# Attention values of a head group: four runs of one head each, or one run with two heads alternating in the two column halves

## Chip, cores and metric

One core of a Trainium2 chip runs the whole program. The metric is the device time in microseconds, as the median of three runs. The chip's engines are named as in the profile: PE (matrix multiply; PEld is its weight load), DVE (vector), ACT (activation), POOL, and SP, which issues most loads.

## What is computed

One layer of a transformer trunk for 256 tokens of width 1024: a sparse-attention mixer, a cross attention to 256 memory tokens, and a convolutional feed-forward network. The change lies in the mixer, which has 16 heads of width 64 in 4 groups. The four heads of a group share keys and values. Cut to what matters:

```python
p_cmp = masked_softmax(einsum('bghtd,bngd->bghtn', qg, k_cmp), cmp_end[None, :] <= t[:, None])
o_cmp = einsum('bghtn,bngd->btghd', p_cmp, v_cmp)
...
p_sel = masked_softmax(einsum('bghtd,bgtkd->bghtk', qg, k_g), ...)
o_sel = einsum('bghtk,bgtkd->btghd', p_sel, v_g)
...
p_win = masked_softmax(einsum('bghtd,bkgd->bghtk', qg, k_w), wmask)
o_win = einsum('bghtk,bkgd->btghd', p_win, v_w)
o = g_blk[..., 0:1] * o_cmp + g_blk[..., 1:2] * o_sel + g_blk[..., 2:3] * o_win
return o.reshape(B, S, D_MODEL) @ w_out
```

With 256 tokens all four key blocks are selected and the window is longer than the sequence, so the selected and the window branch both reduce to causal attention, each with its own keys and values.

## The kernel before, in words

The weights stream from memory in halves of 128x1024 (`load_half`, L108, issued by SP). Each half is split into a high part on ACT (L116) and a low part on DVE (L120), and each weight product takes three PE passes (`mm3`, L183 to L185). At most four halves are in flight as `raw`, six as `hi` and as `lo`.

The attention is cut into units `(g, t)`: a group of four heads and a tile of 128 queries. `UNITS` (L887) lists the eight units, `heads` (L888) the 32 heads `(g, t, i)` in that order. A head of query tile 0 sees 128 keys in two branches (256 columns, two blocks), one of tile 1 sees 256 keys (512 columns, four blocks). A head runs through these steps of the class `Head` (L767):

- `scores`, PE, L779 and L780, into a bank of the tag `S` (two banks);
- `biggest`, DVE, L790: minus the scores and their largest, into `pp` (three buffers);
- `exp`, ACT, L796, twice (one per branch);
- `weigh`, DVE, L801 to L804: the division by the sum and the gate;
- `transposed`, PE, L810, one transpose per block, into a bank of the tag `PT` (two banks);
- `copied`, ACT, L814, from that bank into the tile `pT`, of which there are two buffers;
- `values`, PE, L827, one `matmul` per block: the stationary operand is the block's values, 128 keys by 64 columns, and the moving one is 128 columns of `pT`;
- `summed`, L834: after the unit's fourth head, ACT (L188) and DVE (L192) split the output bank into `oT`.

The output of a unit is one bank of the tag `O` (two banks), 256 columns wide. An even head of the group goes to partitions 0 to 63, an odd one to partitions 64 to 127, the first two heads to columns 0 to 127 and the last two to the rest. So the values of an even head occupy one half of the PE array's columns and those of an odd head the other half. Ahead of the first head's values, two products over all 128 columns (L821) put the compressed branch of all four heads into the bank. All operands here are float32: each such `matmul` is issued as two pairs of a weight load and a matmul, so the 96 calls of L827 stand as 192 matmuls in the profile.

The loop at L893 staggers the heads: in step `n` it issues the scores of head `n`, the weighing of head `n-1`, the transposes and copy of head `n-2`, and the values of head `n-3`. Between them `advance` (L878) takes steps from other products: the remaining queries, the memory's keys (`pmk`) and values (`pmv`). The output projection that follows (`residual`, L917, `pr_out` in the profile) uses `oT`.

That is the program's order, and it isn't the order on the engines. In this stretch only SP and POOL keep the written order (`M2`, L891). For PE, ACT and DVE a planner fixes one order per engine when the kernel is built: it goes by costs that it models, prefers what stands earlier in the program, and takes whatever is ready in its model. On the chip each engine then follows that fixed order and waits where it must.

Of the kernel before, what the change touches and what calls it, by code (L numbers as in the profile page):

```python
# [17 lines left out]
P = 128  # L18
# [16 lines left out]
# columns of the per-partition constants  # L35
# [7 lines left out]
def trunk_kernel(ctx: ExitStack, tc: tile.TileContext, a, out):  # L43
# [60 lines left out]
    def load_half(i):  # L104
        """Load the next half of chunk i."""
        h = len(raws.setdefault(i, []))
        raw = wpool.tile([P, NHALF], F32, tag="raw", name=f"raw{i}_{h}", bufs=RAW)
        nc.sync.dma_start(raw, chunks[i][0][:, h * NHALF:(h + 1) * NHALF])  # L108
        raws[i].append(raw)

    def split_half(i, lo=None):
        """Split the next half of chunk i, or the one part of it."""
        if not lo:
            h = len(his.setdefault(i, []))
            his[i].append(wpool.tile([P, NHALF], F32R, tag="hi", name=f"hi{i}_{h}", bufs=NBUF))
            nc.scalar.activation(his[i][h], raws[i][h], AF.Copy)  # L116
        if lo is not False:
            h = len(parts.setdefault(i, []))
            t = wpool.tile([P, NHALF], F32R, tag="lo", name=f"lo{i}_{h}", bufs=NBUF)
            nc.vector.tensor_tensor(t, raws[i][h], f(his[i][h]), op=ALU.subtract)  # L120
            parts[i].append((his[i][h], t))

    def half(i, h, k):
        """Half h of chunk i, of which the rows-tile k comes next; what follows has been split up to
        AHEAD halves on."""
        if not order:
            order.extend((n, j) for n, c in enumerate(chunks) for j in range(c[1] // NHALF))
        at = order.index((i, h))
        at += min(AHEAD, RAMP + (at - 4) // RS)
        while state["hi"] < len(order) and state["hi"] <= at:  # L130
            n, j = order[state["hi"]]
            if len(raws.get(n, [])) == j:
                load_half(n)
            split_half(n, False)
            state["hi"] += 1
        while state["lo"] < state["hi"] and (state["lo"] < at or k >= SKEW):
            split_half(order[state["lo"]][0], True)
            state["lo"] += 1
        return parts[i][h]

    def wtile(i, k, c, n):
        """hi and lo of rows-tile k, columns c:c+n of a chunk [P, 8, 256]."""
        hi, lo = half(i, k // 4, k % 4)
        o = (k % 4) * 256 + c
        return hi[:, o:o + n], lo[:, o:o + n]

    def wrow(i, k):
        """hi and lo of rows-tile k (of 4) of a chunk [P, 4, 512]."""
        hi, lo = half(i, k // 2, 2 * (k % 2))
        o = (k % 2) * 512  # L150
        return hi[:, o:o + 512], lo[:, o:o + 512]

    # the order in which the chunks are used
# [26 lines left out]
    def mm3(ps, lw, rx, start, stop):  # L180
        """Three float32r passes of a float32 product: hi hi, hi lo, lo hi."""
# [14 lines left out]
    def split(*items):  # L196
        """hi + lo = src (* scale), each of float32r, for (hi, lo, src, scale): all of one bank,
        which one engine reads at a time."""
# [6 lines left out]
    def sumsq(src, nm, dve=False):  # L205
        """The sum of the squares of src over D."""
# [8 lines left out]
    def partial(parts_, nm):  # L215
        """eps and the sums of squares but the last."""
# [20 lines left out]
    def across(rs, row, nm, tag="O"):  # L237
        """rs [tokens, tiles] as a row of tokens, the same in all partitions."""
# [39 lines left out]
    def proj_ws(ps, ci, ct, pair, t=None):  # L278
        """ps[128 columns of the weights, tokens] of chunk ci, column tile ct."""
# [3 lines left out]
    def proj_ws_steps(ps, ci, ct, pair):  # L283
        """The same in steps, between which other products can go."""
# [4 lines left out]
    def proj_as(ps, c0, pair, t):  # L289
        """ps[tokens of t, 512 columns] from the two chunks c0, c0 + 1."""  # L290
# [3 lines left out]
    # products of a stream come in steps, between which other pieces of work go  # L294
# [10 lines left out]
    def between(stream, start):  # L305
        """The steps of the stream, and of the work that starts at the given ones."""
# [17 lines left out]
    # the memory's keys and values, at the other end of the memory  # L324
# [4 lines left out]
    with tc.tile_pool(name="attn", bufs=1, reuse_waits="tile") as at:  # L329
# [10 lines left out]
        hT = act_pair("hT", "aA")  # L340
        # the root mean squares of the tokens scale what comes out of the products with x
        xT = act.tile([P, KT, S], F32, tag="aB_hi", name="xT")
        rs_x = at.tile([P, NT], F32, name="rs_x")
        with tc.manual_schedule():
# [11 lines left out]
            # the table of the functions is loaded, and the clock of the PE array rises, while the first  # L356
            # loads arrive
# [24 lines left out]
        # queries: rows of hi and lo of one head  # L382
        QS = at.tile([P, G, HPG, S], F32R, name="QS")
        with tc.tile_pool(name="cmp", bufs=1, side="right", reuse_waits="tile") as cp:
# [8 lines left out]
            def rms():  # L393
                """The root mean squares of the tokens: per token, and as a row; then the values."""
# [19 lines left out]
            # ---- compressed keys' and values' inputs: [(parity, d), position pair, part, (chunk, group)],  # L414
            # for the first and the second half of a block; the last column is the position embedding ----
# [71 lines left out]
            gel = cp.tile([P, 2, 2, NC], F32, name="gel")  # L487

            def hidden(j, then):
                """Twice the gelu of the hidden layer, [hidden, (block, group)]."""  # L490
# [47 lines left out]
            def gated():  # L538
                """The gates."""
# [76 lines left out]
            def compressed_values():  # L616
                # block-diagonal over the four heads of a group
# [39 lines left out]
        with tc.tile_pool(name="aq", bufs=1, reuse_waits="tile") as aq:  # L657
# [18 lines left out]
            def mem_values(h):  # L676
                """The values of head h."""
# [87 lines left out]
            # all of the four blocks are selected, and the window is longer than the sequence, so the  # L765
            # masks of these two branches are the causal one
            class Head:  # L767
# [14 lines left out]
                def biggest(self):  # L782
# [5 lines left out]
                    # minus the scores (scaled by the queries' rms), and minus their largest  # L788
# [23 lines left out]
                def copied(self):  # L812
                    self.pT = aq.tile([P, 512], F32, tag="pT", name=f"pT{self.name}", bufs=2)
                    nc.scalar.activation(self.pT[:, :self.w], self.pt[:, :self.w], AF.Copy)  # L814

                def values(self):
                    g, t, i = self.g, self.t, self.i
                    if i == 0:
                        Os[g, t] = bank("O", f"O{g}{t}")
                        for m in range(2):  # L820
                            nc.tensor.matmul(Os[g, t][:, m * P:(m + 1) * P], Vc[:, g, m, :], pcT[:, g, t, :],  # L821
                                             start=m == 0, stop=False, skip_group_check=True)
                    O = Os[g, t]
                    po = O[(i % 2) * DK:(i % 2) * DK + DK, (i // 2) * P:(i // 2 + 1) * P]
                    nb = 2 * (1 + t)
                    for blk in range(nb):
                        nc.tensor.matmul(po, V[:, blk // 2, blk % 2, g, :], self.pT[:, blk * P:(blk + 1) * P],  # L827
                                         start=False, stop=i == HPG - 1 and blk == nb - 1,
                                         skip_group_check=True)
# [32 lines left out]
            def fill():  # L862
                """The steps of other products."""
# [24 lines left out]
            heads = [Head(g, t, i) for g, t in UNITS for i in range(HPG)]  # L888
            for t in range(NT):
# [27 lines left out]
    def residual(c0, pair, nm, norm, man):  # L917
        """x += pair @ w; norm(t, sums of squares of the halves) of each tile of tokens."""
# [23 lines left out]
    with tc.tile_pool(name="cross", bufs=1, reuse_waits="tile") as cr:  # L942
# [8 lines left out]
        def cross_q(ci, ps):  # L951
            """The queries of head ci, transposed."""
# [7 lines left out]
        def cross_p(h):  # L960
            """The probabilities of head h, transposed."""
# [37 lines left out]
        # the first heads' queries by tiles of tokens, then transposed  # L999
# [33 lines left out]
    with tc.tile_pool(name="ffn", bufs=1, reuse_waits="tile") as fp:  # L1033
# [5 lines left out]
        # the first pairs of column tiles by tiles of tokens, then transposed  # L1039
# [42 lines left out]
        def add_pd(pd, t, h, c0, c1):  # L1082
            """x += pd for columns c0:c1 of half h, and the sum of squares."""
# [6 lines left out]
        for h in range(2):  # L1090
            # (tokens, columns) of the accumulators
# [27 lines left out]
def _rows(w, c0, c1):  # L1119
    """[K, c0:c1] -> [128, K / 128, c1 - c0]: rows of a tile on the partitions."""  # L1120
# [4 lines left out]
def _stationary(w):  # L1125
    """Chunks of 256 columns and all rows."""
# [3 lines left out]
def _moving(w):  # L1130
    """Chunks of 512 columns and 512 rows, the columns outermost."""
# [4 lines left out]
def _moving_r(w):  # L1136
    """The same, the rows outermost."""
# [71 lines left out]
```

## Time and profile before

| what | value |
|---|---|
| device time, median of 3 runs | 483.68 us (483.61 to 483.83) |
| span of the profiled execution, from its first to its last instruction | 481.1 us |
| PE busy | 464.0 us, 96% |
| DVE busy | 328.6 us, 68% |
| ACT busy | 294.0 us, 61% |
| values (L827), busy on PE, 192 matmuls | 27.4 us |

The page of the profile gives the profiled execution's span; the device time of the runs holds a little more than a span, what lies ahead of the first and behind the last instruction. An instruction that PE shows as busy overlaps its neighbours, since matmuls are pipelined: two matmuls can start 0.11 us apart and be shown with 0.27 us each. What a matmul costs is therefore read from the distance between starts, not from its shown length.

### The profile page before, as it was taken

What the parts mean: (1) busy time and instruction counts of PE and PEld (TensorE: products, weight loads), DVE (VectorE), ACT (ScalarE), POOL (GpSimd) and SP (SyncE); (2) the same over time, 40 slices, a digit from 0 to 9 for tenths busy, and PEclk for the clock granted to TensorE, in tenths of its full rate; (3) what the DMA queues carried; (4) which work ended last, traced back from release to release, by engine and by line L of the source; (5) the groups of instructions that cost most, each with busy time, mean ns of one, the idle gap of its engine ahead of it and who ended that gap; (6) DMA issues with size and microseconds to landing.
All of it is one profiled execution on the core that took longest, in us unless ns stands there. A gap on an engine that the chain in (4) does not pass through costs nothing.

```text
span 481.1 us, 8742 instructions
## 1 busy us (share of the span) xinstructions
PE 464.0 (96%) x3278; PEld 423.7 (88%) x3278; DVE 328.6 (68%) x716; ACT 294.0 (61%) x613; POOL 37.5 (8%) x82
## 2 busy tenths in 40 slices
PE   7999598999999999999999999999999999999994
PEld 4899598899988777789999889999999999888884
DVE  4799879688777668485563395897777777744413
ACT  5889769666677567484555275766666666534401
POOL 4122101211100000010000010000000000000203
PEclk9999978999999999999999999999999999999998
DMA  7987785432222200264533453765555555654502
GB/s 265 359 272 254 216 281 199 164 131 89 104 74 88 89 1 1 90 201 158 196 104 117 143 178 124 235 211 190 188 190 176 177 176 176 215 179 137 169 0 89
DMA packets 22074, 77.05 MB, mean 160 GB/s; under 512 B 2704, under 2 KB 3088, under 8 KB 22032
## 3 DMA queue, kind: packets, MB, share of 16 engines
q1 hardware_dynamic: 21312, 74.65, 45.6%
q10 hardware_dynamic: 720, 1.84, 1.1%
q8 instruction: 26, 0.43, 0.4%
q14 instruction: 16, 0.13, 0.1%
HBM read 75.43 MB, written 1.05 MB: 159 GB/s over the span
## 4 chain that ended last, share of the span: by engine, by line
PE 85%; DMA 6%; DVE 3%; ACT 2%; issue 2%; SPq 0%; POOLq 0%; ACTq 0%; DVEq 0%; POOL 0%
PE up L183 8%; PE up L185 8%; PE up L184 8%; PE O L827 5%; PE pd L183 4%; PE pd L184 4%; PE pd L185 4%; DMA raw<-in_w_q 3%; PE pt L810 3%; DMA raw<-in_w_vsvw 2%; PE pmk L183 2%; PE pmk L185 2%; PE pmv L185 2%; PE pr_out L183 2%; PE pmv L183 2%
## 5 line engine op out<-in xcount | busy, mean ns | idle before, releaser
L120 DVE TENSOR_TENSOR lo<-raw,hi 128x1024 fp32r<-128x1024 f32 x134 | 164.0, 1230 | 64.6 <-ACT hi L116 63.9
L116 ACT ACTIVATE hi<-raw 128x1024 fp32r<-128x1024 f32 x134 | 141.5, 1059 | 67.6 <-PE pd L185 17.7
L183 PE MATMUL up<-h_hi,hi 128*128 128x256 f32 x304 | 86.1, 283 | 0.0
L185 PE MATMUL up<-h_hi,lo 128*128 128x256 f32 x304 | 86.0, 283 | 0.0
L184 PE MATMUL up<-h_lo,hi 128*128 128x256 f32 x304 | 86.0, 283 | 0.0
L184 PEld LDWEIGHTS up<-h_lo,hi 128*128 128x128 f32 x304 | 58.4, 192 | 0.0
L185 PEld LDWEIGHTS up<-h_hi,lo 128*128 128x128 f32 x304 | 58.4, 192 | 0.0
L183 PEld LDWEIGHTS up<-h_hi,hi 128*128 128x128 f32 x304 | 58.4, 192 | 0.0
L185 PE MATMUL pd<-hi,aT_lo 128*128 128x512 f32 (+1 forms) x110 | 38.4, 349 | 0.0
L184 PE MATMUL pd<-lo,aT_hi 128*128 128x512 f32 (+1 forms) x110 | 38.4, 349 | 0.0
L183 PE MATMUL pd<-hi,aT_hi 128*128 128x512 f32 (+1 forms) x110 | 38.4, 349 | 0.0
L790 DVE CUSTOM_DVE_ANT_0 pp<-s,tri,nrs 128x128 f32<-128x128 f32 (+1 forms) x64 | 24.2, 414 | 13.0 <-PE pt L810 8.0
L796 ACT ACTIVATE pp<-pp,nm 128x128 f32<-128x128 f32 (+1 forms) x64 | 28.4, 447 | 5.1 <-DVE nm L790 4.9
L827 PE MATMUL O<-pT,V 128*64 128x128 f32 x192 | 27.4, 281 | 0.0
L814 ACT ACTIVATE pT<-pt 128x256 f32<-128x256 f32 (+1 forms) x32 | 15.5, 488 | 17.9 <-PE pt L810 17.8
L827 PEld LDWEIGHTS O<-pT,V 128*64 128x64 f32 x192 | 19.7, 136 | 6.4 <-ACT pp L796 1.6
L183 PEld LDWEIGHTS pd<-hi,aT_hi 128*128 128x128 f32 x110 | 20.7, 188 | 2.9
L185 PEld LDWEIGHTS pd<-hi,aT_lo 128*128 128x128 f32 x110 | 20.7, 188 | 2.9
L184 PEld LDWEIGHTS pd<-lo,aT_hi 128*128 128x128 f32 x110 | 20.7, 188 | 2.9
L1069 ACT ACTIVATE th<-c 128x256 f32<-128x256 f32 x22 | 9.1, 414 | 22.2 <-DVE c L1067 22.2
L183 PE MATMUL pq<-hT_hi,hi 128*128 128x256 f32 x64 | 19.1, 299 | 0.4 <-DVE QS L584 0.4
L804 DVE TENSOR_SCALAR pp<-pp,den 128x128 f32<-128x128 f32 (+1 forms) x64 | 18.5, 329 | 0.8
(305 smaller groups left out, 1162.0 us busy)
## 6 DMA issues: line engine op xcount, KB each, us to landing
raw<-in_w_up SPq DMA_DIRECT2D x44, 512.0 KB, 4.3
raw<-in_w_dn SPq DMA_DIRECT2D x20, 512.0 KB, 3.6
raw<-in_w_q SPq DMA_DIRECT2D x8, 512.0 KB, 6.0
raw<-in_w_mk SPq DMA_DIRECT2D x8, 512.0 KB, 5.2
raw<-in_w_mv SPq DMA_DIRECT2D x8, 512.0 KB, 3.5
raw<-in_w_out SPq DMA_DIRECT2D x8, 512.0 KB, 3.6
raw<-in_ca_wq SPq DMA_DIRECT2D x8, 512.0 KB, 4.0
raw<-in_ca_wo SPq DMA_DIRECT2D x8, 512.0 KB, 4.0
```

What stands on the lines that cost most here:

```text
L116: nc.scalar.activation(his[i][h], raws[i][h], AF.Copy)
L120: nc.vector.tensor_tensor(t, raws[i][h], f(his[i][h]), op=ALU.subtract)
L183: nc.tensor.matmul(ps, lh, rh, start=start, stop=False)
L184: nc.tensor.matmul(ps, lh, rl, start=False, stop=False)
L185: nc.tensor.matmul(ps, ll, rh, start=False, stop=stop)
L790: nc.vector.tensor_tensor_reduce(self.ppv[:, br], sv[:, br], tri[:, 1 - t:], nrs[:, t:t + 1], 3e38, ALU.add, ALU.min, self.nm[:, br:br + 1])
L796: nc.scalar.activation(self.ppv[:, br], self.ppv[:, br], AF.Exp, bias=self.nm[:, br:br + 1], scale=-1.0, accum_out=self.den[:, br:br + 1])
L804: nc.vector.tensor_scalar(self.ppv[:, br], self.ppv[:, br], den[:, br:br + 1], None, op0=ALU.mult)
L810: nc.tensor.transpose(self.pt[:, o:o + P], self.pp[:, o:o + P], ident)
L814: nc.scalar.activation(self.pT[:, :self.w], self.pt[:, :self.w], AF.Copy)
L827: nc.tensor.matmul(po, V[:, blk // 2, blk % 2, g, :], self.pT[:, blk * P:(blk + 1) * P], start=False, stop=i == HPG - 1 and blk == nb - 1, ...
L1069: nc.scalar.activation(th, c, AF.Tanh, scale=0.5)
```

## The change

`copied` has six buffers of `pT` where it had two. `values` does nothing for the first three heads of a group. For the fourth it allocates the unit's bank, issues the compressed branch's two products, and then the values of all four heads: first those of heads 3 and 2, block by block and in turns, then those of heads 1 and 0. `heads[n].n` is the head's place in the list, so that the fourth head finds the others. (Comments that the change drops are not shown.)

```diff
                 def copied(self):
-                    self.pT = aq.tile([P, 512], F32, tag="pT", name=f"pT{self.name}", bufs=2)
+                    self.pT = aq.tile([P, 512], F32, tag="pT", name=f"pT{self.name}", bufs=6)
                     nc.scalar.activation(self.pT[:, :self.w], self.pt[:, :self.w], AF.Copy)
 
                 def values(self):
-                    g, t, i = self.g, self.t, self.i
-                    if i == 0:
-                        Os[g, t] = bank("O", f"O{g}{t}")
-                        for m in range(2):
-                            nc.tensor.matmul(Os[g, t][:, m * P:(m + 1) * P], Vc[:, g, m, :], pcT[:, g, t, :],
-                                             start=m == 0, stop=False, skip_group_check=True)
-                    O = Os[g, t]
-                    po = O[(i % 2) * DK:(i % 2) * DK + DK, (i // 2) * P:(i // 2 + 1) * P]
+                    if self.i < HPG - 1:
+                        return
+                    g, t = self.g, self.t
+                    O = Os[g, t] = bank("O", f"O{g}{t}")
+                    for m in range(2):
+                        nc.tensor.matmul(O[:, m * P:(m + 1) * P], Vc[:, g, m, :], pcT[:, g, t, :],
+                                         start=m == 0, stop=False, skip_group_check=True)
+                    group = heads[self.n - HPG + 1:self.n + 1]
                     nb = 2 * (1 + t)
-                    for blk in range(nb):
-                        nc.tensor.matmul(po, V[:, blk // 2, blk % 2, g, :], self.pT[:, blk * P:(blk + 1) * P],
-                                         start=False, stop=i == HPG - 1 and blk == nb - 1,
-                                         skip_group_check=True)
+                    for m in (1, 0):
+                        for blk in range(nb):
+                            for i in (2 * m + 1, 2 * m):
+                                r = (i % 2) * DK
+                                nc.tensor.matmul(O[r:r + DK, m * P:(m + 1) * P], V[:, blk // 2, blk % 2, g, :],
+                                                 group[i].pT[:, blk * P:(blk + 1) * P], start=False,
+                                                 stop=blk == nb - 1, skip_group_check=True)
...
             heads = [Head(g, t, i) for g, t in UNITS for i in range(HPG)]
+            for n, h in enumerate(heads):
+                h.n = n
```

## Rows read from the trace of the kernel before

**Rows 1.** Page, parts 1 and 4: busy time; chain that ended last, by engine.

```profile
span 481.1 us, 8742 instructions
PE 464.0 (96%) x3278; PEld 423.7 (88%) x3278; DVE 328.6 (68%) x716; ACT 294.0 (61%) x613; POOL 37.5 (8%) x82
...
PE 85%; DMA 6%; DVE 3%; ACT 2%; issue 2%; SPq 0%; POOLq 0%; ACTq 0%; DVEq 0%; POOL 0%
```

**Rows 2.** Stretches of the attention, from:to, length, busy us and count per engine.

```profile
113.00:206.00 93.00, 93.00 (x627) 76.79 (x626) 64.85 (x263) 61.41 (x182) 4.65 (x7) 1.00 0.21 70
113.00:126.00 13.00, 13.00 (x95) 11.29 (x94) 11.11 (x44) 10.00 (x32) 1.49 (x2) 1.00 0.39 136
126.00:157.00 31.00, 31.00 (x243) 27.95 (x242) 22.95 (x94) 21.35 (x63) 1.81 (x2) 1.00 0.21 71
170.00:195.00 25.00, 25.00 (x149) 19.13 (x148) 19.39 (x84) 17.90 (x57) 0.22 (x1) 1.00 0.05 17
```

**Rows 3.** Waits from 92 to 207 us: who for whom, total, times, longest.

```profile
ACT pT L814 <- PE pt L810: 17.8, 21, 2.0
DVE pp L790 <- PE pt L810: 8.0, 10, 1.5
```

**Rows 4.** Groups of instructions, 92 to 207 us: count, busy us, mean ns, idle before.

```profile
L827 PE MATMUL O<-pT,V 128*64 128x128 f32 x192 | 27.4, 281 | 0.0
```

**Rows 5.** Timeline of PE, two runs of values between other work: start, us, what.

```profile
116.85 0.28 PE L184 MATMUL pmk<-memT_lo,hi 128*128 128x256 f32 x1
116.97 0.28 PE L185 MATMUL pmk<-memT_hi,lo 128*128 128x256 f32 x1
117.18 0.65 PE L827 MATMUL O<-pT,V 128*64 128x128 f32 x4
117.76 0.39 PE L183 MATMUL pmk<-memT_hi,hi 128*128 128x256 f32 x1
...
125.63 0.28 PE L184 MATMUL pmk<-memT_lo,hi 128*128 128x256 f32 x1
125.85 1.09 PE L827 MATMUL O<-pT,V 128*64 128x128 f32 x8
126.86 0.39 PE L185 MATMUL pmk<-memT_hi,lo 128*128 128x256 f32 x1
```

**Rows 6.** Timeline, PE and PEld, where two heads' values follow each other.

```profile
137.44 1.12 PEld L827 LDWEIGHTS O<-pT,V 128*64 128x64 f32 x14
137.44 1.36 PE L827 MATMUL O<-pT,V 128*64 128x128 f32 x14
...
138.74 0.33 PE L810 MATMUL pt<-ident,pp 128*128 128x128 f32 x1
...
139.00 0.43 PE L827 MATMUL O<-pT,V 128*64 128x128 f32 x2
```

**Rows 7.** Two stretches of it, L827 alone: PE and PEld busy us, instructions in flight.

```profile
137.45:137.90 0.45, 0.45 (x4) 0.45 (x5) 1.00 0.00 0
137.95:138.40 0.45, 0.45 (x10) 0.45 (x9) 1.00 0.00 0
```

**Rows 8.** Timeline of ACT: the copy of the second of these two heads.

```profile
135.23 0.60 ACT L814 ACTIVATE pT<-pt 128x512 f32<-128x512 f32 x1 [1.01 <-PE pt L810]
```

**Rows 9.** Groups of instructions, 92 to 207 us: one head's steps, query tile 1.

```profile
L796 ACT ACTIVATE pp<-pp,nm 128x256 f32<-128x256 f32 x32 | 15.9, 501 | 0.7 <-DVE nm L790 0.5
L790 DVE CUSTOM_DVE_ANT_0 pp<-s,tri,nrs 128x256 f32<-128x256 f32 x32 | 14.3, 481 | 5.5 <-PE pt L810 4.3 <-PE s L780 1.1
L796 ACT ACTIVATION_READ_ACCUMULATOR pp<-pp,nm 128x1 f32 x64 | 12.2, 190 | 0.0
L804 DVE TENSOR_SCALAR pp<-pp,den 128x256 f32<-128x256 f32 x32 | 10.3, 363 | 0.4
L814 ACT ACTIVATE pT<-pt 128x512 f32<-128x512 f32 x16 | 9.4, 594 | 10.0 <-PE pt L810 10.0
L810 PE MATMUL pt<-ident,pp 128*128 128x128 f32 x96 | 17.4, 280 | 0.0
```

## Prediction, made before the changed kernel was built

> **What bounds the kernel now.** I read the page first, for the engine and the chain: PE is busy 96% of a span of 481.1 us and holds 85% of the chain that ended last [rows 1]. So work taken from PE counts, as long as PE stays the engine that others wait for. Second come the stretches of the attention, since all values lie between 113 and 206 us: there PE is busy for all 93.00 us at a granted clock of 1.00, the upper of its two levels (2.4 GHz), while DVE has 64.85 us and ACT 61.41 us of work [rows 2]. Third, the waits: ACT waits 17.8 us for PE's transposes before copies, and DVE 8.0 us for them before new scores [rows 3], whereas no matmul of the values found PE idle (0.0 in the last column of [rows 4]). PE sets the pace, and the softmax engines follow it. Fourth, the single runs of values, for their true price: PE's shown lengths overlap, so I go by starts.
>
> A run of four matmuls (one head of query tile 0) starts at 117.18, and the work around it starts at 116.97 and 117.76 [rows 5]. Without the run the later start would come 0.12 us after the earlier one, as it does between the matmuls of this size at 116.85 and 116.97 [rows 5]. The run costs 0.79 - 0.12 = 0.67 us. A run of eight (tile 1) costs 126.86 - 125.63 - 0.12 = 1.11 us. Four more matmuls add 0.44 us, 0.11 us each; so a run carries a fixed 0.67 - 4 x 0.11 = 0.23 us (with unrounded steps of 0.109, 0.24), which is paid for going from full-width products to half the columns and back.
>
> **What the change removes.** Before, there are 32 runs, one per head; I listed all: 16 of four and 16 of eight, together 16 x 0.67 + 16 x 1.11 = 28.5 us, less 0.4 us at one place where two runs met (next paragraph): 28.1 us. After, there are 8 runs, four of 16 matmuls and four of 32.
>
> First term, **fewer runs**: 24 x 0.24 = 5.8 us less, if each new run stays whole.
>
> Second term, **two halves at a time**. Whether PE runs an even and an odd head at once is what the sum hangs on, and the trace shows it once: at 137.44 two heads of tile 1 follow each other without other work between. Fourteen matmuls are shown in 1.36 us [rows 6], where eight take 1.09 [rows 5]; six more one behind the other would have made 1.09 + 6 x 0.11 = 1.75. And by the two equal stretches of 0.45 us, 4 matmuls and 5 loads are in flight in the first head's part, 10 and 9 where the heads meet [rows 7]. The second head's `pT` had been copied by 135.83 [rows 8], so it was not the data that came late: the later matmuls went ahead of the earlier head's remaining ones into the other half. Two per 0.11 us it is, about 0.055 us each, and the new order alternates halves after every two, which asks less looking ahead than those fourteen did. The 192 matmuls then take 192 x 0.055 = 10.5 us where they take 192 x 0.109 - 0.4 = 20.5 us: 10.0 us less. The bounds are 0 (no overlap in this order) and 10.0; I take 10.0, from the one row that shows it.
>
> On this point a page speaks against the change: the Trainium skill, "TensorE: Matmul & The Clock Gate", Part 3, says that a weight load overlaps with matmuls in flight only when the two lie in different row groups, and that matmuls are strictly in order. Both halves here use all rows, so by that rule the second term would be nothing. The trace doesn't agree: nine loads are in flight where one half alone had five [rows 7].
>
> Together PE has 15.8 us less, of 93.00: per unit 2.4 us for tile 1 (4 x 1.11 - 32 x 0.055 - 0.24) and 1.6 us for tile 0 (4 x 0.67 - 16 x 0.055 - 0.24). The two full-width products of each unit (L821) only move with the values; they are the same number at the same price, and their place in PE's order is still ahead of a run, so I count 0 for them: both before and after a full-width matmul is next to the run.
>
> **What the change moves, and what it costs.** The values of three heads of each unit go behind the fourth's copy. On PE's order they make room for what stood behind them, and PE has that: fill steps of the memory's products up to 157 us and `pr_out` after it; both stand between the runs now. The copies no longer wait for a buffer: six of `pT` hold a unit's four and the next two. No DMA, no SP or POOL instruction is moved, and DVE and ACT get no new instruction. The fourth head's values end a unit as before, so `oT` comes late by at most the rest of a longer run, 1.98 - 1.11 = 0.9 us, with `pr_out` of other units to cover it. At the last unit it is the next thing PE wants from it, and with that cover gone 0.9 us would be paid once; I take 0, since PE has other groups of `pr_out` and transposes of the next norm there.
>
> Third term, **breaks**: PE's order is the planner's, and it may put transposes or fill steps into a run. It did so in one of 32 runs, between the fourteen and the last two of [rows 6]; each break costs another 0.24 us. The new runs are 1.1 and 2.0 us long where they were 0.7 and 1.1, and the next head's transposes stand ahead of them in the program. Bounds: none, and three in each of 8 runs, 24 x 0.24 = 5.8 us, which is the old number of pieces. I take six, 1.4 us, nearer to the one break seen.
>
> Fourth term, **the softmax engines**. In 113 to 126 us DVE has 11.11 us of work in 13.00; the stretch holds four heads of tile 0 (1.6 us less), so PE would want it done in 11.4. In 170 to 195 us there are six heads of tile 0 and four of tile 1 (6 x 0.40 + 4 x 0.61 = 4.8 us less): 20.2 us for DVE's 19.39. In 126 to 157 us there are five of tile 1 and four of tile 0: 26.4 us for 22.95 [rows 2]. If DVE can get to 100%, nothing is lost; if not above the 11.11 / 13.00 = 85.5% that it shows in the first of them now, the stretches need 13.0, 22.7 and 26.8 us, and 1.6 + 2.5 + 0.4 = 4.5 us are lost. At 92%, midway, it is 12.1 and 21.1 and nothing: 1.6 us. PE would stand idle there and have to wait for a head. DVE's idle time is now mostly waiting for PE, so I stay nearer the middle than the upper end: 2.3 us.
>
> Sum: 15.8 - 1.4 - 2.3 = 12.1 us. All durations are of the profiled execution, whose span of 481.1 us becomes 469.0. The runs' 483.61 to 483.83 lie 2.5 to 2.7 us above that span, which the change doesn't touch: median 483.68 - 12.1 = **471.6 us**.
>
> **Rivals.**
> - *The softmax engines or the planner take more*: both upper bounds, 15.8 - 5.8 - 4.5 = 5.5, gives 478.2; half as bad gives 474.9. For it, DVE's 85% in the first stretch. Against it, the waits that point from PE to DVE and ACT. Chance 0.15, for 474.9 to 478.2.
> - *The halves don't run at once in this order*, because the switch between them after every second matmul has its price, which the trace of before never shows: only the first term stays, 483.68 - 5.8 = 477.9. The fourteen matmuls are one case only, but a plain one. Chance 0.08. (The rule of the Trainium skill named above would give this time too.) That the change doesn't do what it says would be the same number or worse: runs broken into as many pieces as before.
> - *Nothing is left*: breaks take the first term and one of the other costs most of the second; within 0.2%, about 1 us, which is what a measurement of this kernel can tell from no change. Chance 0.05.
> - *Slower: PE waits at the end of each unit.* PE follows a fixed order. If the planner puts a unit's run right behind the fourth head's copy, in the model on time, but on the chip late, all of PE stands behind that wait, the next head's scores too. What would be exposed is at most a head's chain: 2 x 0.48 for L790, 2 x (0.50 + 0.19) for L796, 2 x 0.36 for L804, 0.28 + 3 x 0.11 for L810, 0.59 for L814 [rows 9], 4.3 us in all; eight times that, 34 us. The change turns slower above 15.8 / 8 = 2.0 us per unit. At 2.5 us it is 8 x 2.5 - 15.8 = 4.2 us slower, 487.9. Against it, each of 32 runs waits for a copy now, and none left PE idle [rows 4]. Chance 0.07.
>
> **How the numbers follow.** The forecast's own case has 0.65, with 467.9 (15.8 with no loss) to 474.9. Faster by over 0.2%: 0.65 + 0.15 + 0.08 = 0.88; within: 0.05; slower: 0.07. The range begins a little under the forecast's lower bound, 467.4, and must reach over the two rivals up to 478.2: 479.0, which leaves out the last two cases, 0.12, and some of the edges.
>
> **What would show it.** Eight runs of L827 (some broken) instead of 32, a run of 32 within about 2.0 us, and twice as many of its matmuls and loads in flight as in a head alone; if a run of 32 takes 3.6 us, the halves don't overlap. DVE's share between 113 and 195 us near 90%, PE still with hardly any idle time. The part behind the attention should be as long as before. I'd be wrong if PE shows waits for `pT` or for `pp` of a microsecond and more in front of the runs, if the runs are in many pieces, or if the granted clock falls in the stretch because PE idles.

## The result, and the profile after

The changed kernel takes 470.46 us (median of four runs, 469.05 to 470.97) against 483.75 us (483.61 to 484.44): a ratio of 0.9728, with a 95% interval of 0.9706 to 0.9751. It is 13.3 us faster; 12.1 had been forecast.

The page of the changed kernel, parts 1 and 4 (busy time; the chain that ended last, by engine), to be read beside [rows 1]:

```profile
span 468.5 us, 8741 instructions
PE 449.5 (96%) x3278; PEld 415.1 (89%) x3278; DVE 326.8 (70%) x716; ACT 293.9 (63%) x613; POOL 37.6 (8%) x82
...
PE 83%; DVE 6%; DMA 6%; ACT 2%; issue 2%; POOLq 0%; DVEq 0%; SPq 0%; POOL 0%; ACTq 0%
```

The span is 12.6 us shorter and PE's busy time 14.5 us, with the same 3278 matmuls. PE still has 83% of the chain, and DVE's share has doubled to 6%: the first sign that the softmax now comes into sight.

The stretches of the attention after (the columns as in [rows 2]):

```profile
113.00:126.00 13.00, 13.00 (x113) 12.44 (x111) 12.80 (x52) 10.07 (x32) 1.47 (x2) 1.00 0.47 148
126.00:157.00 31.00, 31.00 (x256) 28.64 (x255) 24.53 (x99) 24.60 (x70) 1.46 (x2) 1.00 0.31 103
157.00:190.00 33.00, 31.70 (x234) 25.03 (x233) 26.88 (x117) 24.77 (x78) 0.22 (x1) 1.00 0.12 41
```

DVE is busy for 12.80 of 13.00 us in the first, 98%, and PE waits for nothing there. In the last PE is idle for 1.3 us, where it had not been idle at all. The waits between 92 and 200 us (who for whom, total, times, longest) name the place:

```profile
ACT pT L814 <- PE pt L810: 11.0, 15, 2.6
DVE pp L790 <- PE pt L810: 3.3, 3, 1.7
...
PE s L779 <- DVE den L801: 1.2, 3, 0.7
```

The waits for PE of [rows 3] are smaller (17.8 and 8.0 before), and a new one points the other way: PE waits 1.2 us for DVE before new scores. The values themselves found PE idle for 0.1 us (the group of L832, 92 to 200 us, as in [rows 4]):

```profile
L832 PE MATMUL O<-pT,V 128*64 128x128 f32 x192 | 13.1, 278 | 0.1
```

The timeline of PE shows a whole run and a torn one, and below them stand the instructions of L832 in flight (PE, PEld) in a stretch of the whole one that is as long as those of [rows 7]:

```profile
135.44 0.65 PE L832 MATMUL O<-pT,V 128*64 128x128 f32 x6
136.02 0.33 PE L810 MATMUL pt<-ident,pp 128*128 128x128 f32 x1
136.28 0.43 PE L832 MATMUL O<-pT,V 128*64 128x128 f32 x2
136.64 0.33 PE L810 MATMUL pt<-ident,pp 128*128 128x128 f32 x1
136.90 1.53 PE L832 MATMUL O<-pT,V 128*64 128x128 f32 x24
...
178.66 1.97 PE L832 MATMUL O<-pT,V 128*64 128x128 f32 x32
180.55 0.50 PE L183 MATMUL pr_out<-hi,oT_hi 128*128 128x512 f32 x1
```

```profile
179.00:179.45 0.45, 0.45 (x12) 0.45 (x10) 1.00 0.00 0
```

Thirty-two matmuls are shown in 1.97 us, where eight took 1.09 [rows 5]. Twelve matmuls and ten loads are in flight in 0.45 us, against 4 and 5 of one head alone [rows 7]. By the starts in the trace, an odd head's matmul and an even head's begin 5 to 8 ns apart, and the next such pair 109 ns after the last (the second pair of a run 160 ns). In all there are 11 pieces: eight runs and three breaks, two of them in the torn run above.

Where the time went is seen best from the distance between matmul starts, given to the tile that the first of the two writes, and added up from the first `pst` to the first `up`. Both kernels do the same matmuls between those two.

```
us, start to start     before    after
O (values, L821)         28.7     15.7
pmk                      24.6     24.0
pmv                      24.5     24.1
pr_out                   23.9     23.0
pt_cross                  2.0      1.8
s (scores)               13.3     14.0
pt (transposes)          10.1     10.4
all others               79.4     79.4
sum                     206.5    192.4
```

The values, with their two full-width products, give 13.0 us. Another 2.1 us lie on their neighbours (`pmk`, `pmv`, `pr_out`, `pt_cross`): that is the way into a run, which a start-to-start count gives to the matmul ahead of it. Scores and transposes took 1.0 us back. From the first matmul of `up` to the end both kernels need 191.2 us.

The distance of 14.1 us is more than the 12.6 of the spans, because the front differs: the first `pst` starts at 83.4 us in the profiled execution before and at 84.9 after. Over all kernels of this study it starts between 82.0 and 85.4 us, with the same matmuls in the same order up to it; that spread sits in PE's waits (in front of `pkc` 1.4 us before and 4.1 after) and in the stretches at the lower clock (1.2 GHz), the last of which ahead of `pst` ends at 82.2 us at the latest. So in the table below the distance from the first `pst` to the first matmul of `up` on L183 stands beside each time, as a measure without the front.

### The profile page after: what moved, and what is told of

The parts are those of the page before. It is cut to its first block, busy times and chain, and to the rows that moved or that the text cites. A ratio compares the mean times of both kernels' runs of the same rounds, so it can differ in the third digit from the quotient of the medians.

```text
span 468.5 us, 8741 instructions
## 1 busy us (share of the span) xinstructions
PE 449.5 (96%) x3278; PEld 415.1 (89%) x3278; DVE 326.8 (70%) x716; ACT 293.9 (63%) x613; POOL 37.6 (8%) x82
## 4 chain that ended last, share of the span: by engine, by line
PE 83%; DVE 6%; DMA 6%; ACT 2%; issue 2%; POOLq 0%; DVEq 0%; SPq 0%; POOL 0%; ACTq 0%
PE up L185 8%; PE up L184 8%; PE up L183 8%; PE pd L184 4%; PE pd L183 4%; PE pd L185 4%; DMA raw<-in_w_q 3%; DVE lo L120 3%; PE O L832 2%; PE pt L810 2%; PE pmk L183 2%; PE pcq L183 2%; PE pmk L184 2%; PE pmv L184 2%; PE pmv L183 2%
## 5 line engine op out<-in xcount | busy, mean ns | idle before, releaser
L183 PE MATMUL up<-h_hi,hi 128*128 128x256 f32 x304 | 86.2, 283 | 0.0
L183 PEld LDWEIGHTS up<-h_hi,hi 128*128 128x128 f32 x304 | 58.4, 192 | 0.0
L183 PE MATMUL pd<-hi,aT_hi 128*128 128x512 f32 (+1 forms) x110 | 38.4, 349 | 0.0
L183 PEld LDWEIGHTS pd<-hi,aT_hi 128*128 128x128 f32 x110 | 20.7, 188 | 2.9
L183 PE MATMUL pq<-hT_hi,hi 128*128 128x256 f32 x64 | 19.0, 297 | 0.4 <-DVE QS L584 0.4
L185 PE MATMUL pq<-hT_hi,lo 128*128 128x256 f32 x64 | 19.0, 296 | 0.0
L184 PE MATMUL pq<-hT_lo,hi 128*128 128x256 f32 x64 | 18.9, 295 | 0.0
```

The costliest lines, as they stand in the source:

```text
L183: nc.tensor.matmul(ps, lh, rh, start=start, stop=False)
L184: nc.tensor.matmul(ps, lh, rl, start=False, stop=False)
L185: nc.tensor.matmul(ps, ll, rh, start=False, stop=stop)
```

## The experiments

The kernel before ran again beside each group of experiments: medians of 483.26, 483.27 and 482.55 us. The ratios are to these. "Pieces" are the uninterrupted stretches of value matmuls, runs and parts of broken runs alike.

| kernel | us | ratio to before, interval | `pst` to `up`, us | pieces |
|---|---|---|---|---|
| before | 483.75 | | 216.7 | 32 |
| changed | 470.46 | 0.9706 to 0.9751 | 202.6 | 11 |
| halves apart | 476.24 | 0.9823 to 0.9888 | 209.0 | 10 |
| heads in turn | 470.99 | 0.9718 to 0.9779 | 204.5 | 10 |
| two runs | 470.08 | 0.9686 to 0.9750 | 202.9 | 16 |
| buffers alone | 484.02 | 0.9996 to 1.0029 | 216.7 | 32 |
| split run | 471.75 | 0.9722 to 0.9783 | 204.3 | 16 |
| less on DVE | 466.39 | 0.9619 to 0.9685 | 199.2 | 8 |
| before, less on DVE | 483.07 | 0.9981 to 1.0011 | 216.4 | 33 |
| 28 steps first | 467.27 | 0.9647 to 0.9703 | 200.6 | 8 |
| before, 28 steps | 486.43 | 1.0049 to 1.0107 | 219.4 | 33 |
| 24 steps first | 467.95 | 0.9647 to 0.9731 | 202.0 | 9 |
| two runs, 28 steps | 468.92 | 0.9669 to 0.9739 | 203.0 | 16 |
| 32 steps first | 468.17 | 0.9651 to 0.9737 | 202.5 | 8 |

**Halves apart: is it the overlap?** The run stays one, but the odd half's heads go first, then the even half's.

```diff
-                    for m in (1, 0):
+                    for i in (3, 1, 2, 0):
+                        m, r = i // 2, (i % 2) * DK
                         for blk in range(nb):
-                            for i in (2 * m + 1, 2 * m):
-                                r = (i % 2) * DK
...
```

> The same one run per unit, but heads in the order 3, 1, 2, 0: the odd half of the columns first, all its matmuls one behind the other, then the even half. If the two halves at a time are worth about 10 us: they meet only once per unit, about 0.39 us saved at each of 8 meetings, so 192 x 0.109 - 3.1 = 17.8 us of values where the changed kernel has 10.5: 7.3 us slower than it, 477 to 479 us. If the gain comes from the fewer runs and the freed buffers, and the overlap is hidden or worth nothing: 470 to 471.5 us.

476.24 us, 5.8 us slower than the changed kernel, and 6.4 by the distance: nearly what the overlap was to be worth, though a little under the range. The timeline of PE in this kernel:

```profile
182.67 3.33 PE L831 MATMUL O<-pT,V 128*64 128x128 f32 x32
185.93 0.50 PE L183 MATMUL pr_out<-hi,oT_hi 128*128 128x512 f32 x1
```

The same 32 matmuls, with the same runs around them, take 3.33 us where they took 1.97. Its values take 22.6 us from start to start, 6.9 more than alternating. The two halves still meet once per run, and by the starts each of the 8 meetings saves 0.38 us against one matmul per 0.109 us. So the whole overlap is worth 6.9 + 8 x 0.38 = 9.9 us (9.4 with the 6.4 of the whole distance in place of the 6.9 of the values).

**Heads in turn: how far does PE look ahead?** The same edit with another order.

```diff
-                    for i in (3, 1, 2, 0):
+                    for i in (3, 2, 1, 0):
```

> One run per unit, heads in the order 3, 2, 1, 0, each with all its blocks: the halves alternate after 8 or 4 matmuls instead of 2. If PE's looking ahead spans some three matmuls, as where two heads met in the kernel before, all but the first few of a head overlap with its neighbour: about 0.1 to 0.45 us per unit more than when alternating, 471 to 474 us. If it needs the alternation after every block: as with the halves apart, 477 to 479 us.

470.99 us, at the lower edge of the first range, and 1.9 us more than the changed kernel by the distance. By the starts, where a head has four matmuls the next head's first begins 14 ns after its own first; where a head has eight, it begins with the fifth. Either way a matmul for the free half passes just three that wait for the other half. The timeline shows what that leaves of a run of 32:

```profile
179.17 2.57 PE L831 MATMUL O<-pT,V 128*64 128x128 f32 x32
181.67 0.50 PE L183 MATMUL pr_out<-hi,oT_hi 128*128 128x512 f32 x1
```

That is 0.60 us more than alternating for a whole run of tile 1; for a run of tile 0 it is 0.05. The change's order, two by two, stays inside what PE looks past.

**Two runs and a split run: what does a run cost?** In the first, heads 0 and 1 run after head 1, and heads 2 and 3 after head 3:

```diff
-                    if self.i < HPG - 1:
+                    if self.i % 2 == 0:
                         return
...
+                    for blk in range(nb):
+                        for h in (heads[self.n], heads[self.n - 1]):
+                            r = (h.i % 2) * DK
```

> Two runs per unit instead of one: heads 0 and 1 after head 1, heads 2 and 3 after head 3, alternating as in the changed kernel. If a run has a fixed price of 0.24 us: 8 more of them are 1.9 us, less what the planner breaks less often (up to 3 x 0.24): 471.5 to 472.5 us. If waiting for the fourth head costs more than the longer run saves: 470 us or less.

470.08 us: between the two ranges, so a miss. It is no slower than one run, though not faster either by the distance (202.9 against 202.6). The 16 runs stayed whole, so only five more pieces stand against the changed kernel's 11, and PE was idle for 0.6 us in place of 1.3. Five pieces at 0.24 us are 1.2 us, and of that 0.7 came back as idle time that PE no longer had; 0.5 would be left, and the distance shows 0.3. In the split run the waits are kept: a full-width product moves between the two pairs of heads.

```diff
-                    for m in range(2):
-                        nc.tensor.matmul(O[:, m * P:(m + 1) * P], Vc[:, g, m, :], pcT[:, g, t, :],
-                                         start=m == 0, stop=False, skip_group_check=True)
...
                     for m in (1, 0):
+                        nc.tensor.matmul(O[:, m * P:(m + 1) * P], Vc[:, g, m, :], pcT[:, g, t, :],
+                                         start=m == 1, stop=False, skip_group_check=True)
                         for blk in range(nb):
```

> The changed kernel with one of the two full-width products moved between the two pairs of heads, so that each unit's run falls in two, with the same matmuls and the same waits. If going from full width to half the columns and back costs 0.24 us each time: 8 x 0.24 = 1.9 us slower than the changed kernel, 472 to 473 us, and in the profile the distance from start to start on these matmuls grows by about as much. If the switch is free and only the overlap counts: 470 to 471 us.

471.75 us, 1.3 slower than the changed kernel and 1.7 by the distance; the first range began a little higher. Its timeline:

```profile
178.92 1.09 PE L831 MATMUL O<-pT,V 128*64 128x128 f32 x16
179.95 0.49 PE L826 MATMUL O<-pcT,Vc 128*128 128x128 f32 x2
180.37 1.09 PE L831 MATMUL O<-pT,V 128*64 128x128 f32 x16
181.39 0.50 PE L183 MATMUL pr_out<-hi,oT_hi 128*128 128x512 f32 x1
```

From 178.92 to 181.39 are 2.47 us; in the changed kernel the whole run takes 180.55 - 178.66 = 1.89, and the two matmuls between are 2 x 0.109 = 0.22 of the rest. So the extra switch costs 0.36 us here, more than the 0.24 of [rows 5]. A run's price isn't one number: it depends on what lies beside it. But a float32 product of full width isn't by itself a dearer neighbour than a weight product. The kernel before has a run between float32 transposes:

```profile
132.93 0.60 PE L810 MATMUL pt<-ident,pp 128*128 128x128 f32 x4
133.46 1.09 PE L827 MATMUL O<-pT,V 128*64 128x128 f32 x8
134.47 0.66 PE L810 MATMUL pt<-ident,pp 128*128 128x128 f32 x4
```

Four transposes and eight matmuls take 134.47 - 132.93 = 1.54 us to the next start; at 0.109 each they would take 1.31. The price is 0.23, within rounding the 0.24 between weight products. What comes on top in the split run is that the pair in between stands alone: by the starts its second matmul begins 0.213 us after the first, not 0.109. Nor is it the change from weight products to float32 that costs: in the kernel before, three weight products and two single transposes between the PE starts at 119.15 and 119.73 take 0.58 us, which is 3 x 0.12 + 2 x 0.11. So the price belongs to the half columns. The Trainium skill, "TensorEngine Tiling (Array Packing)", Key Properties, says that a change of the tiling mode drains the engine, without a price; these prices fit it, though the trace doesn't show the drain itself.

**Buffers alone**, on the kernel before:

```diff
-                    self.pT = aq.tile([P, 512], F32, tag="pT", name=f"pT{self.name}", bufs=2)
+                    self.pT = aq.tile([P, 512], F32, tag="pT", name=f"pT{self.name}", bufs=6)
```

> The kernel before with six buffers of the transposed probabilities in place of two, nothing else. If the buffers only make the late values possible: the time before, 482.7 to 484.7 us. If copies that waited for a buffer held PE up: part of the gain already, below 482 us.

484.02 us, and the same distance to 0.1 us. The buffers are what the late values need, and no gain.

**Less on DVE: does the softmax bound it now?** The weighing takes the gate alone, in both kernels:

```diff
-                    den = self.den
-                    nc.vector.reciprocal(den, den)
-                    nc.vector.tensor_tensor(den, den, gates[:, self.g, self.t, self.i, 1:3], op=ALU.mult)
+                    den = gates[:, self.g, self.t, self.i, 1:3]
```

> The changed kernel without the two small DVE instructions per head that divide by the sum (L801, L802; the weighing then uses the gate alone, so the division is left out of the result): about 10.6 us of DVE work less, and a shorter chain per head. If PE is still the bound and the softmax engines cost only the 1.3 us in which PE shows idle in front of scores: 0.5 to 1.5 us faster than the changed kernel, 469 to 470.5 us, with hardly any idle time of PE left between the first scores and the last values. If DVE has become the bound there: 3 us or more, below 467.5 us.

> The kernel before without the same two DVE instructions per head (the division by the sum is left out of the result). PE had no idle time there, so 10.6 us less on DVE are worth nothing: 483 to 484.5 us. If the softmax engines held it up already: below 482 us.

On the kernel before it changes nothing (0.9981 to 1.0011). On the changed kernel it is worth 4.1 us, 3.4 by the distance: beyond the first range and, by the time, inside the one for DVE as the bound. (DVE's busy time falls by 6.6 us, less than the 10.6 of instruction lengths, which overlap; on the kernel before it falls by 7.3.) By the starts, 1.0 us of it is gone from the scores (PE's idle time), 1.7 from the transposes and 0.9 from the values: the planner, with less to plan on DVE, left all eight runs whole, and transposes no longer stand singly between pieces of a run. DVE isn't the bound in the sense that its work sets the time; it was busy for 64.21 us of 77 between 113 and 190 us in the changed kernel, and 57.89 of 74 between 113 and 187 us here. Its work costs PE's order some 3 us. How much of that is the wait on the chip and how much the planner's order, this kernel doesn't separate, since the edit changes both.

**28, 24 and 32 steps ahead of the heads.** `FIRST`, the steps of other products that stand ahead of the first head, goes from 36 to 28, on both kernels, and to other values:

```diff
-            FIRST, TAIL, RATIO = 36, 2, 0.8
+            FIRST, TAIL, RATIO = 28, 2, 0.8
```

> The changed kernel with 28 instead of 36 steps of other products ahead of the first head, so that eight steps more (24 matmuls, 2.9 us of PE) are left to lie between the heads. If the 1.3 us of idle time of PE come from a lack of such work beside the softmax of the later heads: up to 1 us faster, 469.3 to 470.5 us. If the planner's order of the heads sets them: no change, 470 to 471 us; a start of the heads ahead of the weights could cost up to 1 us.

> The kernel before with 28 instead of 36 steps ahead of the first head, the control for the same edit on the changed kernel (467.3 us there). If those 3 us came from what the change brought, fewer breaks in the long runs and room beside the softmax engines: no change here, 482.5 to 484.5 us. If the eight steps are better placed in any case: about 480 us.

> The changed kernel with 24 steps ahead of the first head. If whole runs are what the 28 steps brought: the same as with 28 where the runs stay whole, 466.5 to 468 us, and 0.5 to 0.7 us more for each break that comes back. If the room beside the softmax engines counts: about 1 us less than with 28, 466 to 467 us.

> The changed kernel with 32 steps ahead of the first head. If the time goes by the breaks of the runs: 467 us with none, 0.5 to 0.7 us more for each, up to the changed kernel's 470.5 with three. If it goes by the steps left beside the softmax engines: halfway, about 469 us, whatever the breaks.

> Two runs per unit and 28 steps ahead of the first head. With 36 steps two runs showed no breaks and the time of the changed kernel. If whole runs are what 28 steps brought: nothing to win here but the 0.6 us in which PE was idle, 469 to 470.5 us, 2 us behind the one run with 28 steps. If it is the room beside the softmax engines: about 467.5 us.

With 28 steps the changed kernel takes 467.27 us, 3.2 us less and so a larger gain than either range had; by the distance it is 2.0 us: the values give 0.9 of it and the transposes 1.1, while PE's idle time stays. A run in it, whole, where the changed kernel had the torn one:

```profile
134.61 1.97 PE L832 MATMUL O<-pT,V 128*64 128x128 f32 x32
136.50 0.44 PE L810 MATMUL pt<-ident,pp 128*128 128x128 f32 x2
```

On the kernel before the same edit costs 3.9 us, which neither range had (2.7 by the distance; PE is idle for 2.1 us there, 1.4 of it behind the attention, in front of `pcqt`). So the gain belongs to the new order. But whole runs aren't the rule behind it: with 32 steps all eight runs are whole too, and the distance is 202.5 us, as in the changed kernel, with 2.2 us of idle time. With 24 steps it is 202.0, and two runs with 28 steps give 203.0 where they had 202.9. Of the ranges, 24 steps (one break) lie in the one for whole runs, 32 steps and two runs in none. These three kernels gained 2.5, 2.3 and 1.2 us in time against the same kernels with 36 steps, but 1.2, 1.2 and 0.7 us of it are already in the kernel before, which was faster beside them, and the distance shows only 0.6 and 0.1 us, and for the two runs nothing; in their profiled runs the front came 2.6 to 3.2 us earlier. Only the one run with 28 steps has 2.0 us where the edit works. Its interval (0.9647 to 0.9703) and that of the changed kernel (0.9706 to 0.9751) just don't meet, so it beats both kernels, by little. Of the 1.9 us between 32 and 28 steps 1.1 are idle time of PE (2.2 against 1.2); why the planner's order comes out better with 28 than with 24 or 32 stays open.

## Why the prediction was right

- **What bounds it.** PE set the pace and kept it: 96% before and after. The control with less on DVE shows for the kernel before what had been read from its waits: 10.6 us of DVE instructions less were worth nothing there.
- **Fewer runs**, forecast 5.8 us with the breaks counted apart. The 11 pieces are 21 fewer, 5.0 us at 0.24 each. The price was read in two places with the same neighbours; it is 0.23 between transposes too, and 0.36 for the extra switch of the split run.
- **Two halves at a time**, forecast 10.0 us, the upper bound, from one place in the trace; 9.9 by the run with the halves apart. This was the term on which the sum hung, and the fourteen matmuls of [rows 6] carried it. The rule of the Trainium skill that spoke against it ("TensorE: Matmul & The Clock Gate", Part 3: loads overlap only between different row groups, matmuls strictly in order) doesn't hold here: the halves share all rows, ten loads are in flight in 0.45 us, and a later matmul passes up to three earlier ones.
- **Breaks**, forecast six for 1.4 us: three, 0.7 us at 0.24. The forecast left out that the transposes which tear a run pay too: 136.02 and 136.64 in the torn run stand singly, 0.26 us from start to start where one in a row takes 0.109. That is about the 0.3 us on `pt`.
- **The softmax engines**, forecast 2.3 us: PE is idle for 1.3 us. The ceiling of 85.5% for DVE, the lossy end, was too low: DVE reached 98% between 113 and 126 us with no loss. The loss came later, in front of scores.
- **Moved values**: counted at nothing, and rightly. The wait of L832 for its last copy is within the 0.1 us of idle time, and after the attention both kernels need the same time.

In sum 15.8 - 0.7 - 1.3 = 13.8 us, against 14.1 from start to start. The forecast had taken 3.7 us off for breaks and softmax where 2.0 were due, so for the stretch that the change touches 12.1 was too little. The runs' times show 13.3 us and the profiled spans 12.6, since they hold the front too, whose start of `pst` lies anywhere in 3.4 us. That the times come nearer to 12.1 than the stretch does is chance; that the gain is made of these terms is not. Of the rivals, no overlap would have given 477.9 and a run of 3.6 us; the run has 1.97. The slower one needed 2.0 us of waiting at each unit's end.

## What to carry to other kernels

Where two products fill different halves of the PE array's columns, issue them in short turns (two matmuls each here; eight in a row lost a part of it) and next to each other: here that alone was worth 9.9 us of the 14. Look for a place in the trace where two such runs already meet, and count starts, not busy time. When the bounding engine's work shrinks, its order among the other engines' work is worth another look: by the distance, a change of `FIRST` that cost the kernel before 2.7 us took 2.0 off the changed one.

## What was not expected of the hardware

A matmul for the free half of the columns passes exactly three waiting ones, whether the other half has four, eight or sixteen in a row (it starts 14 ns after the first, with the fifth, and with the thirteenth). Going from full width to half the columns and back costs 0.24 us, between weight products and between transposes alike; a pair of full-width matmuls alone between two runs costs 0.36. By the starts, 0.09 to 0.10 of the 0.24 lie ahead of a run's first matmul, 0.05 behind the first (0.160 us to the next in place of 0.109) and 0.09 behind the last (0.203).
